# Output products of three mixers, their last two column chunks taken by halves of the tokens, with the next norm and first product also by halves

## The chip, the cores and the metric

The kernel runs on one core of a Trainium2 chip. The metric is the device time of one execution in microseconds (us), the median of several executions. An engine's name in the profile is short: PE is the matrix engine (PEld its weight loads), DVE the vector engine, ACT the scalar engine, POOL the general engine, SP the engine that issues most transfers.

## The reference

Two networks run one after the other over 512 tokens of 1024 features, in 32-bit floats. Cut to what matters here, the order of work is this:

```python
h, gate = adaln_norm(x, ...)                 # mixer 1: norm, scale and shift
x = x + gate * (nsa_mixer(h) @ w_out)        # 16 heads, three branches
h, gate = adaln_norm(x, ...)                 # mixer 2
x = x + gate * (dilated_mixer(h) @ w_out)    # 16 heads in three groups
x = rms_norm(x, final_g)                     # end of the first network
h = modulate(rmsnorm(x, g1), shift1, scale1) # mixer 3: window attention and a short convolution
x = x + gate1 * (merged @ w_out)
h2 = modulate(rmsnorm(x, g2), shift2, scale2)
x = x + gate2 * peer(h2, ...)                # 16384 experts, 8 heads x 16 picked for each token
```

Each norm needs the sum of squares over all 1024 features of a token, so all four column chunks of the output product before it. A token's norm needs nothing of the other tokens.

## The kernel before, in words

Tokens are four tiles of 128 (`NT`), features eight blocks of 128 (`KD`), weights come in chunks of 256 columns (`CW`). The running `x` stays on the chip with tokens on the partitions. Every operand of a large product is split into a high and a low part, and `mm3` (L229) issues three matmuls for one block of 128 features: high with high, high with low, low with high (L230 to L232). A weight chunk is fetched by `load_raw` and split by `load_split` (L220): the high part on ACT (L225), the low part, as raw minus high, on DVE (L226). The split parts live in a pool of two (`wsp`), the raw chunks in a pool of three.

The builder doesn't keep the order in which the program is written: a planner arranges each engine's instructions by a time that it computes for itself, keeping the data's dependences. `behind(...)` (L174) adds an order by hand: an instruction is issued after a named earlier one of its engine. `load_split` uses it for its two instructions unless `wait=False`: they stay behind the last square sum ("stats"), the last split of the norm ("scaled") and, in mixer 3, behind the last split of the convolution branch ("hi" on ACT, "scaled" on DVE, L1105).

The stretch between two mixers, called a join below, is made of three parts:

- The output product of the mixer before: `proj_out` (L446) for mixer 1, loops at L926 for mixer 2 and L1132 for mixer 3. For each of four column chunks c and each token tile t there are 24 matmuls of 256 columns (27 in mixer 2, whose three head groups are summed apart). The result is scaled by the gate, added to `x` (`add_x`, L439), and ACT sums the squares (L321). For c = 3 and t of 2 or 3, DVE does the adds; else POOL does. In mixer 2, `x` is also multiplied by the final weights (L945) and a second sum of squares follows.
- The norm, `adaln` (L350): `rstd_x` (L323) forms an inverse root with a chain of small DVE instructions, for tiles 0 and 1 and for tiles 2 and 3; `y` is the scaled `x` (L372 on DVE, L370 on ACT); PE transposes y in 128 by 128 blocks (L399, 32 of them); one feature block of all 512 tokens is scaled and shifted on DVE or ACT (L404, L402) and split into the parts `hTh` on ACT (L347) and `hTl` on DVE (L348). The norm ahead of the experts also transposes the first token tile back (L410, L411).
- The first product of the next mixer: two blocks of 24 matmuls of 512 columns (mixer 2 and the experts' queries, `gemm_T`, L234), or four token tiles of 24 matmuls of 256 columns (mixer 3, `gemm_N`, L248). Its weights are split with `wait=False`.

PSUM tiles come from pools: `mm` (two), `ss` (three), `tt` (two, tiles named tps), `oo` (one). `bank(t)` (L244) takes tiles 0 and 1 from mm, 2 and 3 from ss. In mixer 2 the third group's sums of two token tiles share one tps tile (L932).

## Time and profile before

| | us |
|---|---|
| median of 3 runs | 2246.64 |
| lowest and highest run | 2243.02, 2252.53 |
| the profiled execution, device time | 2243.89 |
| its span, first to last instruction | 2241.9 |
| PE busy | 2153.9 (96% of the span) |
| DVE busy | 1726.8 (77%) |
| ACT busy | 993.2 (44%) |
| POOL busy | 583.0 (26%) |

The span lies 2.0 us under the device time. Busy shares are means over the whole span. Times below are microseconds from the start of the span. A matmul's length in a timeline includes the time in the pipe, so the distance between two starts tells the pace.

### The profile page before, as it was taken

The page shows a single profiled execution, that of the slowest core. Times are in us where ns is not written, and L with a number is a line of the kernel's source. Part 1 is how long each engine was busy: PE and PEld are TensorE (multiplying, and loading weights), DVE is VectorE, ACT ScalarE, POOL GpSimd, SP SyncE. Part 2 cuts the span into 40 slices and gives each one's busy share as a digit, 9 for nine tenths or more (in the row PEclk, how much of TensorE's full clock was granted, in tenths as well). Part 3 has the DMA queues.
Part 4 walks back from the last instruction along what each step waited for, and adds up shares of the span by engine and source line. Part 5 has one row for each costly group of instructions (what it writes and reads, how often), then busy time and mean ns, then how long its engine had stood idle before and what let it go on. Part 6 is the DMA issues. An engine that isn't in the chain of part 4 may idle for free.

```text
span 2241.9 us, 33090 instructions
## 1 busy us (share of the span) xinstructions
PE 2153.9 (96%) x12587; PEld 1858.0 (83%) x12587; DVE 1726.8 (77%) x3499; ACT 993.2 (44%) x1756; POOL 583.0 (26%) x385
## 2 busy tenths in 40 slices
PE   6989999999999899989999999899999999999998
PEld 4877776977787787788899999788888888888887
DVE  6676788488765587659899998678777878788785
ACT  4435666344555544353344877533233333333331
POOL 1231100211010711110000002245545536435450
PEclk9999999999999999999999999999999999999999
DMA  7541120145441142134445569899999989999993
GB/s 292 204 154 51 38 76 20 57 155 189 158 161 66 67 153 76 39 111 147 153 150 203 217 260 349 326 371 341 349 327 339 361 309 360 333 332 353 335 355 128
DMA packets 151824, 474.38 MB, mean 212 GB/s; under 512 B 14321, under 2 KB 66417, under 8 KB 128625
## 3 DMA queue, kind: packets, MB, share of 16 engines
q1 hardware_dynamic: 108464, 300.28, 37.4%
q0 software_dynamic: 36864, 134.23, 15.8%
q10 hardware_dynamic: 6336, 37.75, 4.3%
q8 instruction: 99, 1.62, 0.3%
q14 instruction: 61, 0.49, 0.1%
HBM read 429.76 MB, written 41.94 MB: 210 GB/s over the span
## 4 chain that ended last, share of the span: by engine, by line
PE 87%; DVE 6%; ACT 2%; DMA 2%; POOL 1%; issue 1%; SPq 0%; ACTq 0%; DVEq 0%; POOLq 0%
PE mmps L230 15%; PE mmps L232 15%; PE mmps L231 15%; PE sp L232 5%; PE sp L230 5%; PE sp L231 5%; PE sp L493 3%; PE tps L231 3%; PE tps L230 3%; PE tps L232 3%; PE tps L517 2%; PE ob L741 2%; DVE adacc L271 2%; PE ob L230 1%; PE ob L232 1%; PE ob L231 1%
## 5 line engine op out<-in xcount | busy, mean ns | idle before, releaser
L230 PE MATMUL mmps<-hTh,whi 128*128 128x384 f32 (+1 forms) x1656 | 600.8, 364 | 6.1 <-ACT pa L1191 2.5
L231 PE MATMUL mmps<-hTl,whi 128*128 128x384 f32 (+1 forms) x1656 | 596.1, 360 | 3.4 <-DVE hTl L348 3.4
L232 PE MATMUL mmps<-hTh,wlo 128*128 128x384 f32 (+1 forms) x1656 | 594.9, 360 | 1.3 <-DVE wlo L226 1.3
L1204 POOL DMA_INDIRECT rows<-in_un_dram,idx x128 | 205.7, 1607 | 595.3 <-DVE rows L1209 336.0
L230 PEld LDWEIGHTS mmps<-hTh,whi 128*128 128x128 f32 x1656 | 312.4, 189 | 38.4 <-ACT pa L1191 3.7
L231 PEld LDWEIGHTS mmps<-hTl,whi 128*128 128x128 f32 x1656 | 313.0, 189 | 31.6 <-DVE hTl L348 5.1
L232 PEld LDWEIGHTS mmps<-hTh,wlo 128*128 128x128 f32 x1656 | 312.5, 189 | 29.4 <-DVE wlo L226 1.6
L225 ACT ACTIVATE whi<-wr 128x2048 fp32r<-128x2048 f32 x121 | 230.2, 1903 | 142.1 <-PE mmps L231 90.3
L226 DVE TENSOR_TENSOR wlo<-wr,whi 128x2048 fp32r<-128x2048 f32 x111 | 252.7, 2277 | 35.5 <-ACT whi L225 35.0
L1204 POOL DMA_INDIRECT rows<-in_v_dram,idx x128 | 198.7, 1552 | 212.1 <-DVE acc L1223 170.0
L1461 DVE TENSOR_TENSOR vl<-wr,vh 128x2048 fp32r<-128x2048 f32 x64 | 146.5, 2290 | 124.7 <-ACT vh L1452 112.0
L1452 ACT ACTIVATE vh<-wr 128x2048 fp32r<-128x2048 f32 x64 | 122.4, 1915 | 258.4 <-PE ob L232 240.2
L271 DVE SCALAR_TENSOR_TENSOR adacc<-wr,c_c,adacc 128x256 f32<-128x256 f32 x308 | 164.5, 552 | 3.2
L1223 DVE SCALAR_TENSOR_TENSOR acc<-rows,dots,acc 128x1024 f32<-128x1024 f32 x127 | 162.6, 1280 | 1.6
L1209 DVE SCALAR_TENSOR_TENSOR rows<-rows,hn 128x1024 f32<-128x1024 f32 x128 | 153.1, 1217 | 7.7 <-DMA rows<-in_un_dram,idx 7.5
L230 PE MATMUL sp<-vh,wh 128*128 128x512 f32 x384 | 144.9, 394 | 10.0 <-ACT wh L1464 10.0
L231 PE MATMUL sp<-vl,wh 128*128 128x512 f32 x384 | 148.7, 393 | 0.0
L232 PE MATMUL sp<-vh,wl 128*128 128x512 f32 x384 | 136.8, 390 | 0.4 <-DVE wl L1465 0.4
L1464 ACT ACTIVATE wh<-pa 128x768 fp32r<-128x768 f32 x64 | 53.1, 842 | 153.6 <-DVE pa L1463 94.5
L231 PE MATMUL tps<-vl,wh 128*128 128x512 f32 x256 | 100.0, 393 | 0.0
L230 PE MATMUL tps<-vh,wh 128*128 128x512 f32 x256 | 98.5, 393 | 0.0
L232 PE MATMUL tps<-vh,wl 128*128 128x512 f32 x256 | 95.0, 389 | 0.0
(1100 smaller groups left out, 4196.8 us busy)
## 6 DMA issues: line engine op xcount, KB each, us to landing
wr<-in_u_dram SPq DMA_DIRECT2D x64, 1024.0 KB, 7.3
wr<-in_v_dram SPq DMA_DIRECT2D x64, 1024.0 KB, 8.3
wr<-in_aw_dram SPq DMA_DIRECT2D x48, 1024.0 KB, 6.6
gd<-stg ACTq DMA_DIRECT2D x12, 2048.0 KB
pg<-gd SPq DMA_DIRECT2D x32, 768.0 KB, 9.7
wr<-in_dilw_dram SPq DMA_DIRECT2D x16, 1024.0 KB, 4.8
ad<-aout ACTq DMA_DIRECT2D x32, 384.0 KB, 2.8
pa<-ad SPq DMA_DIRECT2D x32, 384.0 KB, 9.2
```

The costliest lines, as they stand in the source:

```text
L225: A.activation(hi[:, :, :n], r[:, :, :n], AF.Copy)
L226: (lo_eng or V).tensor_tensor(lo[:, :, :n], r[:, :, :n], hi[:, :, :n].bitcast(F32), op=ALU.subtract)
L230: TE.matmul(ps, sh, mh, start=first, stop=False)
L231: TE.matmul(ps, sh, ml, start=False, stop=False)
L232: TE.matmul(ps, sl, mh, start=False, stop=last)
L271: V.scalar_tensor_tensor(acc, r[:, k, :], m.ccol[:, k:k + 1], acc, op0=ALU.mult, op1=ALU.add)
L493: TE.matmul(sp[j], q, k, start=False, stop=True, skip_group_check=True)
L1204: G.indirect_dma_start(out=r, out_offset=None, in_=table, in_offset=bass.IndirectOffsetOnAxis(ap=ix, axis=0))
L1209: V.scalar_tensor_tensor(r, r, 1.0, hn, op0=ALU.mult, op1=ALU.mult, accum_out=dots[:, n:n + 1])
L1223: V.scalar_tensor_tensor(acc, r, dots[:, n:n + 1], acc, op0=ALU.mult, op1=ALU.add)
L1452: A.activation(vh, vr, AF.Copy)
L1461: paced(V.tensor_sub(vl, vr, vh.bitcast(F32)))
```

## The change

The output product of each of the three mixers keeps chunks 0 and 1 as they were. Chunks 2 and 3 are both loaded and split ahead, and then run for token tiles 0 and 1 (both chunks) and then for tiles 2 and 3. The norm of tiles 0 and 1 is written between chunk 2 and chunk 3 of tiles 2 and 3. The first product of the next mixer is written for the first half of the tokens, then the norm of the second half, then the product of the second half. `adaln_halves` takes the norm's pool while the product before still runs; so the pools of the attention are closed earlier (`ast`), and what outlives them moves (`al`, `fg`, `o5`). The norm writes into the tiles that the output product reads in mixers 1 and 2 (`oT`), at the columns of its own half. `first` holds the first product in two mm tiles until both halves are in. In mixer 2 each token tile takes a tps tile of its own. The chunk-0 split of mixer 3's output product loses its `wait=c > 0`. The back-transposition ahead of the experts becomes `natural`, after the second head's scores. The diff, cut to its core:

```diff
+    def gemm_T_half(hT, w, pss_, half):
+        hs = slice(half * (T // 2), (half + 1) * (T // 2))
+        for b, ps in enumerate(pss_):
+            sl = slice(b * P, (b + 1) * P)
+            for k in range(KD):
+                mm3(ps[:, hs], w[0][:, k, sl], w[1][:, k, sl], hT[0][:, k, hs], hT[1][:, k, hs], k == 0, k == KD - 1)
...
+    def adaln_halves(st, hT, sh, sc, g, fin=False):
+        npool = pool("nrm", 1, st)
+        y = npool.tile([P, NT, D], F32, name="y")
...
+        def half(t0):
+            r, r1 = rstd_x(fin, t0, t0 + 2)
+            for t in (t0, t0 + 1):
+                if t % 2:
+                    A.activation(y[:, t, :], x[:, t, :], AF.Copy, scale=r[:, t - t0:t - t0 + 1])
+                else:
+                    V.tensor_scalar(y[:, t, :], x[:, t, :], r[:, t - t0:t - t0 + 1], None, op0=ALU.mult)
+            hs = slice(t0 * P, (t0 + 2) * P)
+            for k in range(0, KD, 2):
+                src = (pst.tile([P, 2, 2 * P], F32, name="tps", tag="tps") if k % 4 == 0 else pss.tile([P, 2, 2 * P], F32, name="sp", tag="sp"))
+                for j in range(2):
+                    for t in (t0, t0 + 1):
+                        TE.transpose(src[:, j, (t - t0) * P:(t - t0 + 1) * P], y[:, t, (k + j) * P:(k + j + 1) * P], ident)
+                f = npool.tile([P, 2, 2 * P], F32, name="hf", tag="hf", bufs=2)
+                V.tensor_scalar(f[:, 0], src[:, 0], a_[:, k:k + 1], sh.out[:, k:k + 1], op0=ALU.mult, op1=ALU.add)
+                A.activation(f[:, 1], src[:, 1], AF.Identity, scale=a_[:, k + 1:k + 2], bias=sh.out[:, k + 1:k + 2])
+                last["scaled"] = split(hT[0][:, k:k + 2, hs], hT[1][:, k:k + 2, hs], f)
+            if fin:
+                with behind("scaled"):
+                    for t in (t0, t0 + 1):
+                        G.tensor_scalar(x[:, t, :], x[:, t, :], r1[:, t - t0:t - t0 + 1], None, op0=ALU.mult)
+        return half
...
+    def two_halves(wname, step, half):
+        v_ = chunks(i[wname], [CW] * 4)
+        for c in range(2):
+            w = load_split(*v_[c])
+            for t in range(NT):
+                step(t, c, w)
+        w = [load_split(*v_[c]) for c in (2, 3)]
+        for t0 in (0, 2):
+            for c in (2, 3):
+                for t in (t0, t0 + 1):
+                    step(t, c, w[c - 2])
+                if t0 and c == 2:
+                    half(0)
...
-        proj_out(oT, "nsawo", gate.out)
         st.close()
+        half = adaln_halves(nrm, oT, shift[1], scale[1], ng[1])
+        proj_out(oT, "nsawo", gate.out, half)
...
         w0 = load_split(*ch[0], wait=False)
-        hT = adaln(shift[1], scale[1], ng[1])
+        hT = hT1
+        first = [psm.tile([P, T], F32, name="mmps", tag="mm") for _ in range(2)]
+        gemm_T_half(hT, w0, first, 0)
+        half1(2)
+        nrm.close()
...
+        ast.close()
+        half = adaln_halves(st, oT, sh1, sc1, n1g, fin=True)
+        fgp = pool("fgp", 1, st)
+        o5 = [fgp.tile([P, T], F32R, name="o5" + n) for n in "hl"]
+        own_half(o5, zT[:, SPL, :], 1)
+        fg = fgp.tile([P, D], F32, name="fg")
         S.dma_start(fg, i["fg"].to_broadcast([P, D]))
...
-                pa_ = bank(t)
-                if t % 2 == 0:
-                    pb_ = pst.tile([P, T], F32, name="tps", tag="tps")
-                pg = [pa_[:, :CW], pa_[:, CW:], pb_[:, (t % 2) * CW:(t % 2 + 1) * CW]]
+            pa_ = bank(t + 2 * c & 3)
+            pb_ = pst.tile([P, T], F32, name="tps", tag="tps")
+            pg = [pa_[:, :CW], pa_[:, CW:], pb_[:, :CW]]
...
+        two_halves("dilwo", step, half)
+        ch = chunks(i["b2w"], B2_W)
+        w0 = load_split(*ch[0], wait=False)
+        first = [psm.tile([P, T], F32, name="mmps", tag="mm") for _ in range(2)]
+        for t, ps in enumerate(first):
+            gemm_N_tile(oT, w0, CW, ps, t)
+        half(2)
         st.close()
...
-        for c, v_ in enumerate(chunks(i["b2wo"], [CW] * 4)):
-            w = load_split(*v_, wait=c > 0)
+        ast.close()
+        hn_ = new_hT()
+        half = adaln_halves(st, hn_, sh2, sc2, n2g)
...
+        two_halves("b2wo", step, half)
+        w0 = load_split(*chunks(i["wq"], [CW] * 8)[0], wait=False)
+        first = [psm.tile([P, T], F32, name="mmps", tag="mm") for _ in range(2)]
+        gemm_T_half(hn_, w0, first, 0)
+        half(2)
         st.close()
...
+    def natural():
+        for k in range(0, KD, 4):
+            hs = rw.tile([P, 4, P], F32, name="hs", tag="oho")
+            V.tensor_tensor(hs, hT[0][:, k:k + 4, 0:P].bitcast(F32), hT[1][:, k:k + 4, 0:P].bitcast(F32), op=ALU.add)
+            ps = pst.tile([P, T], F32, name="tps", tag="tps")
+            for j in range(4):
+                TE.transpose(ps[:, j * P:(j + 1) * P], hs[:, j, :], ident)
+            A.activation(hn[:, k * P:(k + 4) * P], ps, AF.Copy)
```

## Rows read from the trace of the kernel before

**Rows 1.** The page's chain that ended last: shares of the span by engine

```profile
PE 87%; DVE 6%; ACT 2%; DMA 2%; POOL 1%; issue 1%; SPq 0%; ACTq 0%; DVEq 0%; POOLq 0%
```

**Rows 2.** PE's waits at joins 1, 2, 3: total us, times, longest us

```profile
PE tps L399 <- DVE y L372: 3.5, 2, 3.2
...
PE tps L399 <- DVE y L372: 8.5, 2, 7.7
...
PE tps L399 <- DVE y L372: 4.7, 2, 2.7
```

**Rows 3.** Windows of join 1: PE, PEld, DVE, ACT, POOL busy, PEclk, DMA share, GB/s

```profile
450.00:455.00 5.00, 1.83 (x14) 1.59 (x12) 2.96 (x14) 3.46 (x4) 0.00 (x0) 0.85 0.34 107
455.00:460.00 5.00, 4.95 (x20) 4.16 (x19) 2.92 (x5) 3.24 (x6) 0.00 (x0) 0.50 0.01 3
460.00:465.00 5.00, 5.00 (x26) 4.19 (x25) 3.94 (x6) 3.19 (x6) 0.00 (x0) 0.97 0.23 75
```

**Rows 4.** Timeline, PE, join 1: start us, length us, engine, line, tile

```profile
448.96 0.28 PE L232 MATMUL sp<-whi,hTl 128*128 128x256 f32 x1
...
471.01 0.39 PE L232 MATMUL mmps<-hTh,wlo 128*128 128x512 f32 x1
```

**Rows 5.** Timeline, PE, join 2: last matmuls of chunk 3, tiles 1 and 3

```profile
768.12 0.28 PE L232 MATMUL tps<-whi,hTl 128*128 128x256 f32 x1
...
771.71 0.28 PE L232 MATMUL tps<-whi,hTl 128*128 128x256 f32 x1
```

**Rows 6.** Timeline, DVE and ACT, join 2: y of each half, fourth tile's evacuation

```profile
778.87 0.75 DVE L372 TENSOR_SCALAR y<-x,nr 128x1024 f32<-128x1024 f32 x1
...
782.08 1.15 ACT L370 ACTIVATE y<-x,nr 128x1024 f32<-128x1024 f32 x1 [1.14 <-DVE nr L201]
...
803.40 0.39 ACT L1011 ACTIVATE qk<-mmps 128x256 f32<-128x256 f32 x1 [2.49 <-PE mmps L232]
```

**Rows 7.** Timeline, PE, join 3: end of output product and of first product

```profile
986.01 0.28 PE L232 MATMUL sp<-whi,mTl 128*128 128x256 f32 x1
...
1011.07 0.39 PE L232 MATMUL mmps<-hTh,wlo 128*128 128x512 f32 x1
```

**Rows 8.** The chain in order of time: start us, us, what (joins 1, 2)

```profile
461.90 0.23 PE mmps L232
462.13 0.44 PE sp L399 x4
...
796.63 0.12 PE mmps L231
```

**Rows 9.** Timeline, ACT: second half's y at joins 1 and 3

```profile
453.25 1.15 ACT L370 ACTIVATE y<-x,nr 128x1024 f32<-128x1024 f32 x1 [0.60 <-DVE nr L201]
...
991.89 1.15 ACT L370 ACTIVATE y<-x,nr 128x1024 f32<-128x1024 f32 x1 [0.59 <-DVE nr L201]
```

**Rows 10.** Instructions of tile hf: durations ns, minimum, median, maximum

```profile
L347 ACT ACTIVATE hTh<-hf x32: 612/619/633, 33.9 to 1008.0; 128x512 fp32r<-128x512 f32 x32
L348 DVE TENSOR_TENSOR hTl<-hf,hTh x32: 678/691/1164, 38.7 to 1008.7; 128x512 fp32r<-128x512 f32 x32
```

**Rows 11.** Timeline, ACT and DVE, join 1: split of the next mixer's first weights

```profile
437.76 1.92 ACT L225 ACTIVATE whi<-wr 128x2048 fp32r<-128x2048 f32 x1 [1.02 <-PE sp L232]
...
439.71 2.29 DVE L226 TENSOR_TENSOR wlo<-wr,whi 128x2048 fp32r<-128x2048 f32 x1 [1.45 <-ACT whi L225]
```

**Rows 12.** Timeline, ACT and PE, ahead of mixer 3's output product

```profile
927.89 1.92 ACT L225 ACTIVATE whi<-wr 128x2048 fp32r<-128x2048 f32 x1 [0.41 <-PE mmps L231]
...
939.05 0.39 PE L232 MATMUL mmps<-hTh,wlo 128*128 128x512 f32 x1
...
940.74 0.71 ACT L1102 ACTIVATE mTh<-cy,c_og 128x512 fp32r<-128x512 f32 x1
```

**Rows 13.** Timeline, DVE: group weights of mixer 2 become ready

```profile
730.37 0.17 DVE L920 TENSOR_TENSOR al<-al,gm 128x12 f32<-128x12 f32 x1
```

**Rows 14.** Timeline, POOL, join 2: x scaled by the final norm

```profile
779.73 11.75 POOL L377 TENSOR_SCALAR x<-x,nr 128x1024 f32<-128x1024 f32 x4 [5.05 <-DVE rs_a L197]
```

More of the change, by code (lines that the diff above doesn't have):

```diff
@@ L795, in group_stats, with own_half @@
             V.tensor_scalar(st0[:, :, 1, g], st0[:, :, 1, g], 1.0 / nh, None, op0=ALU.mult)
+        def own_half(dst, f, h):
+            split(dst[0][HS[h]], dst[1][HS[h]], f[HS[h]])
+            for z in dst:
+                A.activation(z[HS[1 - h]], zero[HS[1 - h]].to_broadcast([64, T]), AF.Copy)
         def gated(k):
@@ L800, in gated @@
             if k == SPL:
-                for dst, own, other in ((0, HS[0], HS[1]), (1, HS[1], HS[0])):
-                    hi, lo = [oT[j][:, k, :] if dst == 0 else o5[0][:, j, :] for j in range(2)]
-                    split(hi[own], lo[own], f[own])
-                    for z in (hi, lo):
-                        A.activation(z[other], zero[other].to_broadcast([64, T]), AF.Copy)
+                own_half([z[:, k, :] for z in oT], f, 0)
+                V.tensor_copy(zT[HS[1], k, :], f[HS[1]])
                 return
@@ L821, in ev @@
                     rope_T(tmp, dst[:, b, :], scl, wk, tab, rotr, None if 4 * c + 2 * b < NP else (bycls, inorder))
-                gemm_T(hT, w, 2, ev)
+                if c + cc:
+                    gemm_T(hT, w, 2, ev)
+                else:
+                    gemm_T_half(hT, w, first, 1)
+                    for b in range(2):
+                        ev(b, first[b])
                 ada_next()
@@ L926, in dil, with step @@
[L926 to L927 removed]
+        src = lambda g, k, j: o5[j] if (g, k) == (2, SPL) else oT[j][:, k, :]
+        def step(t, c, w):
             csl = slice(c * CW, (c + 1) * CW)
[L929 to L948 removed]
@@ new lines, in step @@
+            tsl = slice(t * P, (t + 1) * P)
+            pa_ = bank(t + 2 * c & 3)
+            pb_ = pst.tile([P, T], F32, name="tps", tag="tps")
+            pg = [pa_[:, :CW], pa_[:, CW:], pb_[:, :CW]]
+            for g in range(3):
+                for k in rows[g]:
+                    mm3(pg[g], src(g, k, 0)[:, tsl], src(g, k, 1)[:, tsl], w[0][:, k, :], w[1][:, k, :], k == rows[g][0], k == rows[g][-1])
+            tmp = sm.tile([P, CW], F32, name="po", tag="adacc")
+            A.activation(tmp, pg[0], AF.Copy, scale=al[:, t, 0:1])
@@ new lines, in step @@
+            for g in (1, 2):
+                V.scalar_tensor_tensor(tmp, pg[g], al[:, t, g:g + 1], tmp, op0=ALU.mult, op1=ALU.add)
+            eng = V if c == 3 and t >= 2 else G
+            eng.tensor_tensor(tmp, tmp, gate.out[:, csl], op=ALU.mult)
+            add_x(t, c, tmp, eng)
+            eng.tensor_tensor(x[:, t, csl], x[:, t, csl], fg[:, csl], op=ALU.mult)
+            q = square_sum(t, c, 1)
+            if c == 3:
+                last["stats"] = q
+        two_halves("dilwo", step, half)
@@ L1130, in mixer2, with step @@
         rsqrt_(rr, rv, 2 * NT)
[L1132 to L1133 removed]
+        ast.close()
+        hn_ = new_hT()
+        half = adaln_halves(st, hn_, sh2, sc2, n2g)
+        def step(t, c, w):
             csl = slice(c * CW, (c + 1) * CW)
[L1135 to L1149 removed]
@@ new lines, in step @@
+            tsl = slice(t * P, (t + 1) * P)
+            ps = bank(t + 2 * c & 3)
+            pp = [ps[:, :CW], ps[:, CW:]]
+            for hf in range(2):
+                for k in range(4 * hf, 4 * hf + 4):
+                    src = (aT, mT)[hf]
+                    mm3(pp[hf], src[0][:, k % 4, tsl], src[1][:, k % 4, tsl], w[0][:, k, :], w[1][:, k, :], k % 4 == 0, k % 4 == 3)
+            tmp = sm.tile([P, CW], F32, name="po", tag="adacc")
+            A.activation(tmp, pp[0], AF.Copy, scale=rr[:, t:t + 1])
@@ new lines, in step @@
+            t2 = sm.tile([P, CW], F32, name="po", tag="adacc")
+            V.scalar_tensor_tensor(t2, pp[1], rr[:, 4 + t:5 + t], tmp, op0=ALU.mult, op1=ALU.add)
+            t3 = sm.tile([P, CW], F32, name="po", tag="adacc")
+            (V if c == 3 and t >= 2 else G).tensor_tensor(t3, t2, gate.out[:, csl], op=ALU.mult)
+            add_x(t, c, t3, V)
+        two_halves("b2wo", step, half)
+        w0 = load_split(*chunks(i["wq"], [CW] * 8)[0], wait=False)
+        first = [psm.tile([P, T], F32, name="mmps", tag="mm") for _ in range(2)]
@@ L1150, in mixer2 @@
+        gemm_T_half(hn_, w0, first, 0)
+        half(2)
         st.close()
-    mixer2()
+        return hn_, w0, first
+    hT, wq0, first3 = mixer2()
     NH, TK = 8, 16
@@ L1284, in ev @@
             V.tensor_scalar(ids[:, :, m, :], ix, 128.0 if b == 0 else 1.0, None, op0=ALU.mult)
-        gemm_T(hT, w, 2, ev)
+        if h:
+            gemm_T(hT, w, 2, ev)
+        else:
+            gemm_T_half(hT, w, first3, 1)
+            for b in range(2):
+                ev(b, first3[b])
+    def natural():
[6 more added lines that the diff above has]
+            A.activation(hn[:, k * P:(k + 4) * P], ps, AF.Copy)
     def route(t):
@@ L1392, in body @@
         scores(h)
+        if h == 1:
+            natural()
         if h % 2:
```

101 lines of the change are left out of this document (37 added, 64 removed).

## Prediction

> **What bounds the kernel now.** I read the chain that ended last first: 87% of the span is PE [rows 1], so time is won only where PE stands still or runs slowly. PE's waits, asked around the three joins (mixer 1 to 2, 2 to 3, 3 to the experts), show what holds it there: the transposes wait for y, 3.5, 8.5 and 4.7 us [rows 2]. The windows of the first join show a second price: after PE's 3.2 us wait the granted clock goes from 1.0 to 0.85 and then 0.50, that is from 2.4 to 1.2 GHz, and is back at 0.97 only in the window after 460 [rows 3]. So a join is more than its wait; I measure it from the last matmul of the output product to the end of the next mixer's first product.
>
> For the ends I need PE's paces, and the chain in order of time gives them: 0.23 us for a matmul of 512 columns, 0.12 for one of 256, 0.44 for four transposes, so 0.11 each [rows 8].
>
> - Join 1: 448.96 + 0.12 = 449.08 to 471.01 + 0.23 = 471.24 is 22.2 us [rows 4, 8].
> - Join 2: 771.71 + 0.12 = 771.83 to the evacuation of the fourth tile at 803.40, some 0.2 after its last matmul, is 31.4 us [rows 5, 6].
> - Join 3: 986.13 to 1011.30 is 25.2 us [rows 7, 8].
>
> PE's own work in each, at full pace, is 32 transposes (3.5 us) and 48 matmuls of 512 columns (11.0) or 96 of 256 (11.5), and in join 3 eight more transposes (0.9): 14.5, 15.0 and 15.4 us. The joins lose 7.7 + 16.4 + 9.8 = 33.9 us, 1.5% of the time. No change of their order can bring more than that.
>
> **The change part by part.**
>
> *The second half's chain.* With the halves, PE has the first half's product to do (48 matmuls of 256 columns, 48 x 0.12 = 5.8 us) while the second half's norm runs. What ends last is then that norm. From the last matmul to the end of y on ACT before: 453.25 + 1.15 - 449.08 = 5.3 us in join 1, 782.08 + 1.15 - 771.83 = 11.4 in join 2, 991.89 + 1.15 - 986.13 = 6.9 in join 3 [rows 4 to 7, 9]. In join 2 the root chains of both halves stood interleaved on DVE; y of the first half began at 778.87, that of the second at 782.08 [rows 6]. With the first half long done I take 2 us off: 9.4. From y to the first matmul: four transposes 0.44, a scaling of 256 columns out of PSUM about 0.39 (an estimate by the 256-column evacuation on ACT [rows 6]), the high split 0.62 [rows 10], and some 0.3 for hand-overs: 1.8 us. Then 5.8 us of matmuls, and 0.5 because the low part comes 0.69 after the high [rows 10]: 6.3. A pair of blocks costs ACT about 0.39 + 0.62 and DVE about the same + 0.07, under PE's 1.44 for its 12 matmuls, so the split keeps up.
>
> *What the first half adds.* Its 16 transposes (1.8 us) move in front of the join's end; that is no saving, and I add them. Its norm must fit under the product of tiles 2 and 3, four tiles of 2.9 us (3.2 in mixer 2). Queued on DVE in these 11.6 us: the splits and scalings of four pairs (4 x (0.69 + 0.39) = 4.3), a root chain (twelve small steps, of the size of the 0.17 of [rows 13], 2.4 with what lies between them), y (0.75 [rows 6]), eight evacuations and adds of 256 columns (some 3, estimated at 0.39 each), and the next weights' low split (2.29). That last one is what is tight: before, the split of w0 began when chunk 2 let go of its buffer, took 1.92 on ACT and then 2.29 on DVE, and had all of chunk 3, 11.6 us, as cover [rows 11]. Now chunk 2 ends only 5.8 us ahead of the end. ACT and DVE come out at 13 us of work for 13 us of time, so I book 1 us of lateness per join (bounds 0 and 4). In join 2 the first half's y came 778.87 - 768.24 = 10.6 us after its last matmul [rows 5, 6], while only 6.5 us of tiles 2 and 3 of chunk 2 lie between. I book nothing, because the chunk-3 tiles' first two head groups (36 x 0.12 = 4.3 us) need no tps tile and can go first; if they don't, the cost is 4.1 us and a clock that falls.
>
> The joins after: join 1, 1.8 + 5.3 + 1.8 + 6.3 + 1 = 16.2 (gain 6.0); join 2, 1.8 + 9.4 + 1.8 + 6.3 + 1, and 1 for a clock that falls in the some 5 us that stay uncovered = 21.3 (gain 10.1); join 3, 1.8 + 6.9 + 1.8 + 6.3 + 1 = 17.8 (gain 7.4). Together 23.5 us, bounds 14 and 29.
>
> *The lost `wait=c > 0`.* Before, the high split of mixer 3's first output weights ran at 927.89, ahead of the last convolution product, which ended at 939.28; the convolution's high split on ACT came at 940.74 to 941.45 [rows 12]. The new loop keeps every chunk behind that instruction, so this split can't end before 941.45 + 1.9 = 943.35. PE, which went on without a break, has nothing for 943.35 - 939.28 = 4.1 us, more than the wait that brought the clock down in join 1 [rows 2, 3]. Some 4 us of work at 1.2 GHz adds 2. Behind this split stand the low split (DVE, 2.29) and the group of small root steps that the evacuations wait for; four PSUM tiles of work cover those. Cost 6 us, bounds 0 and 8.
>
> *A tps tile for each token tile in mixer 2.* The four third-group sums of chunk 0 fitted into two tiles and ran before their weights `al` were ready at 730.5 [rows 13]; now the third and fourth must wait for an evacuation. 18 x 0.12 = 2.2 us of work can't go ahead; I take 1.5 us, bounds 0 and 3. After that the tiles turn over every 6.5 us, longer than an evacuation behind a low split (some 4).
>
> *Edits at nothing.* `natural` takes 8 transposes out of join 3 and puts them, with two DVE adds, into the scores; PE's work there is the same, and that is in the sum. The two splits at chunk 2 and 3: the second gets its buffer at chunk 1's end and has two tiles, 5.8 us, for 4.2 [rows 11]; without that cover, up to 4 us per mixer. `o5` and `fg` move to memory that attention frees; `fg` is first read after chunk 0, but its transfer stands on SP's queue, where the raw weights go too: 0 if the planner puts it behind them.
>
> *POOL's scaling of x.* It ran from 779.73 for 11.75 us, four instructions of 2.9 [rows 14], beside the second half's chain. DVE's low splits went from 0.69 to at most 1.16 [rows 10]. Now two of the four run in the same place, and I book nothing more. The Trainium skill ("SBUF — State Buffer", "Who interferes with whom") says that a DVE instruction with two SBUF inputs and a GpSimd instruction that reads SBUF exclude one another for the whole instruction; no row here shows such a full block, and the second rival is priced from POOL's row.
>
> The sum: 23.5 - 6 - 1.5 = 16 us off the profiled execution's 2243.9, so 2227.9. The median lies 2.75 above that execution, so 2230.6 on the scale of the median; I say 2230. Nothing later takes it back: a shorter join only starts the experts earlier.
>
> **The rivals.**
>
> 1. *The wait costs nothing* (0.14). The planner had the weights split early and the hand-made order doesn't bind. For it: nothing but the doubt in how the order is kept. 2224.
> 2. *POOL shuts DVE out* (0.05). Both POOL instructions of the first half fall into join 2's second chain and each holds a DVE instruction for up to 2.9 us: 5.8 more, 2236. Against it: the 1.16 above. The page named there would have it so.
> 3. *The first half isn't covered* (0.17). Join 2 pays 4.1 and 3 for the clock, and the three joins are each 1 us later for DVE's queue: 10 us, 2240. For it: the 10.6 us; against it: the two groups that can go first.
> 4. *The planner undoes it* (0.05). It sets the first half's norm behind the whole output product; the joins stay, the two costs come: 2254.
> 5. *Slower: the clock falls twice in each join* (0.07). If PE stands for over 3 us already ahead of the first half's product, waiting for w0 behind DVE's queue, that product runs at 1.2 GHz: 5.8 us more. It is too short to bring the clock back (before, PE worked through the window from 455 to 460 at 0.50 [rows 3]), PE stops again, and the second product pays 5.8 too. 11.6 in three joins less the 1 booked is 34: 2264. It decides at a wait of about 3 us; I have booked 1.
>
> **How the numbers follow.** Some 0.5%, 11 us, is what a measurement of this kernel can tell from no change. The forecast (0.52) and rival 1 lie beyond it on the fast side: 0.66. Rivals 2, 3 and 4 lie within: 0.27. Rival 5: 0.07. The range goes from 2218 (rival 1 with joins at their lower bounds) to 2246 (rival 3 with the wait's upper bound and the tps tiles'), and leaves out rivals 4 and 5 and a little below.
>
> **What the new profile would show.** PE's waits for y at the joins fall from 16.7 us to under 8, almost all at join 2. The joins measure about 16, 21 and 18 us by the same marks. Ahead of mixer 3's output product PE waits some 4 us for an ACT split at L225, with a clock of 0.5 after it. The forecast is wrong if PE waits for L226 or L348 ahead of the first half's product, if the clock is at 0.5 through a whole join, or if transposes of the first half stand on PE waiting while chunk-3 matmuls could run.

## Result, and the profile after

The changed kernel takes 2259.26 us in the median (2255.14 to 2264.94), the kernel before beside it 2246.14: a ratio of 1.0056, interval 1.0040 to 1.0072. It is slower; the forecast was 2230.

The profiled execution of after took 2264.94 us (span 2261.6), the longest of its runs; that of before 2243.89 (span 2241.9). PE's share of the chain that ended last, by engine, went from 87% [rows 1] to 84%:

```profile
PE 84%; DVE 7%; ACT 3%; DMA 3%; issue 2%; POOL 1%; SPq 0%; ACTq 0%; DVEq 0%; POOLq 0%
```

Two profiled executions can't be compared by their clock times: output product 1 begins at 416.8 us before and at 423.0 after, with nothing changed up to there. So I cut both at the same instructions: the first evacuation of output product 1; the first evacuation of mixer 2's key product; the exponential of mixer 2's group weights (`al`); the first evacuation of mixer 3's values; the convolution's last square in mixer 3; the first and the last evacuation of the experts' query scores. Stage lengths in us, with the sum's forecast for each change:

| stage | before | after | change | forecast |
|---|---|---|---|---|
| join 1 | 54.2 | 52.3 | -1.8 | -6.0 |
| middle of mixer 2 | 258.3 | 260.7 | +2.4 | 0 |
| output product 2 and join 2 | 88.7 | 96.4 | +7.7 | -8.6 (10.1 less 1.5) |
| middle of mixer 3 | 122.2 | 125.0 | +2.8 | 0 |
| output product 3 and join 3 | 70.8 | 72.8 | +2.0 | -1.4 (7.4 less 6) |
| scores | 119.5 | 120.4 | +0.9 | 0 |

The changes add up to 14.0 (the medians differ by 13.1), the forecast to -16. Of the 30 us between them 16.3 lie in join 2.

What PE waited for in join 2 and on the way to it, after (total us, times, longest), beside [rows 2]:

```profile
PE tps L446 <- DVE y L440: 9.4, 2, 6.1
...
PE sp L546 <- ACT hf L449: 3.1, 1, 3.1
PE tps L230 <- ACT o5h L867: 2.2, 1, 2.2
...
PE mmps L230 <- ACT qk L1093: 0.7, 1, 0.7
```

The same waits in PE's timeline (start, length, and in brackets the idle time ahead and what ended it):

```profile
737.59 0.58 PE L230 MATMUL tps<-whi,o5h 128*128 128x256 f32 x1 [2.21 <-ACT o5h L867]
...
778.84 0.28 PE L232 MATMUL mmps<-whi,hTl 128*128 128x256 f32 x1
...
785.18 0.47 PE L446 MATMUL tps<-c_ident,y 128*128 128x128 f32 x1 [6.06 <-DVE y L440]
...
793.44 0.28 PE L232 MATMUL tps<-whi,hTl 128*128 128x256 f32 x1
...
808.39 0.58 PE L546 MATMUL sp<-c_masks,c_identb 128*128 128x512 bf16 x1 [3.09 <-ACT hf L449]
...
809.71 0.58 PE L230 MATMUL mmps<-whi,hTh 128*128 128x256 f32 x1 [0.73 <-ACT qk L1093]
```

Windows of after (columns as in [rows 3]): each wait is followed by a stretch in which PE has work at the lower clock, 0.50 being 1.2 GHz.

```profile
735.00:740.00 5.00, 2.79 (x15) 2.71 (x15) 3.71 (x14) 3.42 (x8) 0.00 (x0) 0.59 0.00 0
...
780.00:785.00 5.00, 0.00 (x0) 0.00 (x0) 4.93 (x13) 2.10 (x8) 2.12 (x1) 0.87 0.28 88
785.00:790.00 5.00, 4.82 (x23) 4.83 (x24) 1.90 (x4) 2.69 (x5) 4.78 (x2) 0.50 0.29 123
...
805.00:810.00 5.00, 1.18 (x4) 0.43 (x4) 3.48 (x7) 3.57 (x8) 1.75 (x1) 0.76 0.00 2
810.00:815.00 5.00, 5.00 (x27) 5.00 (x27) 4.76 (x15) 0.04 (x1) 0.00 (x0) 0.55 0.29 79
```

By the forecast's own marks join 2 did shrink: 793.44 + 0.12 = 793.56 to the fourth tile's evacuation at 817.83 is 24.3 us (31.6 before to the same mark; the forecast took 0.2 off). The loss stands ahead of that mark: from the exponential of `al` to the last output matmul it was 771.83 - 729.30 = 42.5, and now 793.56 - 736.02 = 57.5, 15.0 more: the wait for y 6.1, for `o5` 2.2, the first half's 16 transposes 1.8, 16 matmuls of the first product that now run ahead of the mark 1.9, and a rest of 3.0 that I put down to the lower clock.

### The profile page after: what moved, and what is told of

The parts are those of the page before. It is cut to its first block, busy times and chain, and to the rows that moved or that the text cites. A ratio compares the mean times of both kernels' runs of the same rounds, so it can differ in the third digit from the quotient of the medians.

```text
span 2261.6 us, 33325 instructions
## 1 busy us (share of the span) xinstructions
PE 2167.2 (96%) x12683; PEld 1873.9 (83%) x12683; DVE 1733.5 (77%) x3505; ACT 996.1 (44%) x1762; POOL 581.8 (26%) x385
## 4 chain that ended last, share of the span: by engine, by line
PE 84%; DVE 7%; ACT 3%; DMA 3%; issue 2%; POOL 1%; SPq 0%; ACTq 0%; DVEq 0%; POOLq 0%
PE mmps L230 14%; PE mmps L232 14%; PE mmps L231 14%; PE sp L230 5%; PE sp L232 5%; PE sp L231 5%; PE tps L230 3%; PE tps L231 3%; PE sp L552 3%; PE tps L232 3%; PE tps L576 2%; PE ob L800 2%; DVE adacc L284 2%; PE ob L230 1%; PE ob L232 1%
## 5 line engine op out<-in xcount | busy, mean ns | idle before, releaser
L230 PE MATMUL mmps<-hTh,whi 128*128 128x384 f32 (+2 forms) x1688 | 607.2, 361 | 10.3 <-ACT hTh L360 6.1
L231 PE MATMUL mmps<-hTl,whi 128*128 128x384 f32 (+2 forms) x1688 | 603.9, 358 | 5.2 <-DVE hTl L361 5.1
L232 PE MATMUL mmps<-hTh,wlo 128*128 128x384 f32 (+2 forms) x1688 | 602.1, 358 | 2.5 <-DVE wlo L226 2.5
L230 PEld LDWEIGHTS mmps<-hTh,whi 128*128 128x128 f32 x1688 | 319.3, 190 | 42.7 <-ACT hTh L360 7.6
L231 PEld LDWEIGHTS mmps<-hTl,whi 128*128 128x128 f32 x1688 | 320.3, 190 | 33.3 <-DVE hTl L361 7.5
L232 PEld LDWEIGHTS mmps<-hTh,wlo 128*128 128x128 f32 x1688 | 320.1, 190 | 30.9 <-DVE wlo L226 3.3
L1558 ACT ACTIVATE vh<-wr 128x2048 fp32r<-128x2048 f32 x64 | 122.5, 1915 | 286.5 <-PE ob L232 260.2
```

Source lines behind the costliest of these rows:

```text
L230: TE.matmul(ps, sh, mh, start=first, stop=False)
L231: TE.matmul(ps, sh, ml, start=False, stop=False)
L232: TE.matmul(ps, sl, mh, start=False, stop=last)
L1558: A.activation(vh, vr, AF.Copy)
```

## Experiments

### Which join

The theory drawn from these rows was that join 2 alone makes the kernel slower and that the other two gain little; the rivals, that each join loses, or that the lost `wait=c > 0` does. Each join was changed alone, the others written as before, and join 3 also with the wait argument back for the chunk-0 split of mixer 3's output product:

```diff
-            w = load_split(*v_[c])
+            w = load_split(*v_[c], wait=c > 0 or wname != "b2wo")
```

> Only join 1 (mixer 1 to 2) in halves; mixers 2 and 3 and the experts written as before. Theory A, the places: in the two traces join 1 took 1.9 us off, but mixer 2 behind it came out 3.5 us longer with the same work; if that loss belongs to join 1, this kernel is within 3 us of the kernel before (2244 to 2249); if it belongs to join 2's new memory plan, it is 2 us faster than before (2242 to 2245). Theory B, the clock falls twice in each join: a third of the whole loss of 13 us, so 4 us slower (2250).

> Only join 2 (mixer 2 to 3) in halves. Theory A: this is where the time went. From the last of mixer 2's attention to the first evacuation behind the join the trace of after has 7.7 us more than before; 7 to 11 us slower than before (2253 to 2257). Theory B: a third of the loss, 2250.

> Only join 3 (mixer 3 to the experts) in halves, with the first weights of mixer 3's output product kept behind the convolution branch as in after. Theory A: the join wins 4.8 us (25.2 before, 20.4 in the trace of after) and the start of the output product loses about 6: 1 to 3 us slower than before (2247 to 2249). Theory B: 2250.

> As j3_alone, but the first weight chunk of mixer 3's output product is split without the hand-made wait, as in the kernel before. If the lost wait costs what I booked, 6 us, this is 6 us faster than j3_alone, some 4 to 5 us faster than before (2241 to 2243). If the hand-made order does not bind, the two are the same.

| kernel | median us | ratio to before | interval | stage of its join |
|---|---|---|---|---|
| j1_alone | 2246.76 | 1.0002 | 0.9989 to 1.0015 | 52.4 |
| j2_alone | 2258.91 | 1.0050 | 1.0035 to 1.0064 | 96.3 |
| j3_alone | 2248.89 | 1.0008 | 0.9996 to 1.0020 | 72.1 |
| j3_alone_w | 2242.57 | 0.9985 | 0.9976 to 0.9994 | 67.1 |

Join 2 holds the whole loss: 12 us by the medians, more than the 7 to 11 expected. The lost wait costs 6.3 us by the medians and 5.0 by the stage. Join 1's 1.8 us don't reach the end: at about 515 us PE waits 1.2 us in j1_alone for a low split that it didn't wait for before. The same wait in after:

```profile
PE mmps L232 <- DVE wlo L226: 1.3, 1, 1.3
```

### What in join 2

Three causes stood in the rows. (a) The third-group sums of the chunk-3 tiles take tps tiles in the order of the program, behind the first half's transposes, which wait for y; PE, in order, stands with ready work behind it. (b) The first product's tiles 2 and 3 take the two mm tiles of tiles 0 and 1, whose evacuations stand on ACT behind the second half's high splits, and a mask matmul (L546) ahead of them waits for the last `hf`. (c) `o5` is now split behind the exponential of `al` on ACT. One edit for each:

```diff
 (a) j2_sp
-                src = (pst.tile(...) if k % 4 == 0 else pss.tile(...))
+                src = (pst.tile(...) if k % 4 == 0 and not fin else pss.tile(...))
 (b) j2_bank, in the first product of mixer 3
-                ps = bank(0)
+                ps = bank(t if made else 0)
 (c) j2_o5: close ast, take o5 and split it right behind the third group's statistics, ahead of al
```

> Join 2 alone in halves, and o5 with its two splits and two zero copies written ahead of the chain of al, so that ACT's queue has them before al's exp. Theory T3, o5 is late: in the trace of j2_alone PE waits 2.21 us for o5 and then goes at half pace for some 5 us; without it 3 to 5 us less than j2_alone's 2258.9, so 2254 to 2256. Rival R, the time of the join is set by DVE's chain to y alone: the output product ends earlier but y waits for its own squares, which also come earlier; the same 3 to 5. If the third-group sums wait for al anyway, nothing: 2259.

> Join 2 alone in halves, with the transposes of both halves in sp tiles, none in tps. Theory T1, a tps tile blocks: the two third-group sums of chunk 3 (18 matmuls each, 4.3 us) then run ahead of the transposes, into the 5.93 us in which PE waits for y, and the clock falls later or not at all: 5 to 7 us less than j2_alone, 2252 to 2254. Rival R, DVE's chain sets the time: PE gets its 4.3 us of work done and waits the same time later, for the second y; 0 to 2 us less, 2257 to 2259.

> Join 2 alone in halves, with tiles 2 and 3 of the first product in sp tiles, so that they need no evacuation of tiles 0 and 1. Theory T2, the second half's product waits for its tiles: in j2_alone it starts at 805.94 behind waits of 3.09 (for the last hf) and 0.73 us (for the evacuation) and runs at half pace at first; here it can start with the first split pair, some 3 us earlier, and overlap the splits: 3 to 5 us less than j2_alone, 2254 to 2256. Rival R: the same start, 2259.

> The three edits together. If the three waits are separate causes the gains add: 11 to 17 us less than j2_alone, 2242 to 2248, so the same as the kernel before or 5 us faster. If DVE's chain to y sets the time (rival R), only o5's part stays: 2254 to 2256.

> Join 2 alone in halves, with o5's early splits and the transposes in sp tiles, tiles 2 and 3 of the first product as in after. In the traces the stretch from al to the ninth qk evacuation is 99.1 us in j2_alone, 95.7 with o5 early, 94.6 with sp. If the two add, it is 91.2 here, as in the kernel before (91.4), and the time 2246 to 2248. The order of mixer 3's attention is that of the kernel before, so the 15 us that j2_all3's profiled run lost there (clock 0.50 from 882 to 912) should not occur. If that loss comes with join 2 in halves whatever the order, some of the runs are 10 us and more above the rest, as in j2_all3.

| kernel | median us | ratio | interval | join 2's stage |
|---|---|---|---|---|
| j2_alone | 2258.91 | 1.0050 | 1.0035 to 1.0064 | 96.3 |
| j2_o5 | 2254.19 | 1.0023 | 1.0009 to 1.0037 | 93.0 |
| j2_sp | 2249.97 | 1.0006 | 0.9994 to 1.0018 | 91.9 |
| j2_bank | 2249.93 | 1.0006 | 0.9992 to 1.0019 | 90.8 |
| j2_o5_sp | 2251.25 | 1.0024 | 1.0011 to 1.0036 | 87.6 |
| j2_all3 | 2251.25 | 1.0024 | 1.0004 to 1.0045 | 86.2 |

Each cause is real: 3.3, 4.4 and 5.5 us of the stage by itself (by the medians 4.7, 8.9 and 9.0), and 10.1 together where the sum is 13.2.

The wait for the first half's y itself stays: 5.3 us in j2_sp, 7.5 in j2_o5_sp and j2_all3 (7.7 before). What edit (a) gives is that the last output sums no longer stand behind it, so that the second half's y comes 4.2 us earlier after `al`.

With all three the stage is 2.5 below before's 88.7, and the whole kernel isn't faster, against the 2242 to 2248 expected; nor is j2_o5_sp (expected 2246 to 2248), whose stage is 1.1 below before's and whose middle of mixer 3 takes 127.5 us, with PE's order as before. In j2_all3's profiled execution (2260.2; its runs go from 2245.1 to 2266.6) the gain and more went in mixer 3's attention, 139.9 us for 122.2: one wait of 1.9 us for `pt` at 880, and then thirty microseconds in which PE is never idle, at 1.2 GHz:

```profile
872.40:882.40 10.00, 8.13 (x48) 5.64 (x47) 5.54 (x20) 5.73 (x19) 0.00 (x0) 0.96 0.01 2
882.40:892.40 10.00, 10.00 (x30) 5.73 (x29) 5.20 (x22) 3.58 (x15) 0.00 (x0) 0.50 0.28 105
892.40:902.40 10.00, 10.00 (x38) 6.37 (x38) 4.90 (x24) 6.05 (x22) 0.00 (x0) 0.50 0.00 0
902.40:912.40 10.00, 10.00 (x41) 6.26 (x42) 4.73 (x21) 1.11 (x5) 0.00 (x0) 0.50 0.00 0
```

There the planner had ordered the attention differently. But the fall comes without that too, as the next runs show.

### All joins, mended

after_fix3 is the changed kernel with the wait argument back, `o5` early and the transposes in sp tiles alone; j13_w has joins 1 and 3 with the wait argument; j13_w_tiles gives each of a pair's two scalings an output tile and a split of its own:

```diff
-                f = npool.tile([P, 2, 2 * P], F32, name="hf", tag="hf", bufs=2)
+                f0, f1 = [npool.tile([P, 2 * P], F32, name=n, tag=n, bufs=2) for n in ("hf", "hg")]
...
```

> Joins 1 and 3 in halves with the wait restored, join 2 as in the kernel before. If the joins are independent, j1_alone's 0 and j3_alone_w's -4.3 add: 2242 to 2244. If join 2 in halves had been needed by its neighbours or join 1's loss of 1 to 2 us in mixer 2's middle counts, 2245 to 2247.

> As j13_w, but the two scaled blocks of a pair are two tiles with a split each. In join 1 ACT's scaling started when DVE's of the same tile ended (456.31 after 455.73 + 0.54), so the first matmul came 3.4 us after the transposes where I booked 1.8. If the shared tile makes ACT wait, the first matmul of each half comes some 1 us earlier: 2 to 4 us less than j13_w over two joins and two halves, 2238 to 2241. If ACT waits for something else, the four more instructions for a pair cost: 0 to 2 us more than j13_w.

> The kernel after with three edits: the wait restored, o5's splits ahead of al's chain, and the transposes of join 2 in sp tiles. By the single runs, after's 2259.3 less 6.3 (the wait), less 4.7 (o5) and less 8.9 (sp) if all add: 2240; with the two of join 2 adding only to the join's 8 us: 2244 to 2246.

j13_w: 2244.61, 0.9990 (0.9979 to 1.0000). j13_w_tiles: 2243.24, 0.9985 (0.9972 to 0.9997). after_fix3: 2241.68, 0.9981 (0.9968 to 0.9993): faster than both kernels, by 4.5 and 17.6 us. Its stages are 52.3, 259.9, 87.6, 121.4, 68.2 and 120.4; against before that makes 3.9. j13_w_tiles can't be told from j13_w, so the two theories of its expectation stay undecided by the time; its trace is read below.

In the middle of mixer 3, j13_w and j13_w_tiles issue the same instructions in the same order and PE's waits are the same (0.8, 0.8 and 0.9 us); the stage is 122.4 in the one and 125.7 in the other. Two windows of j13_w:

```profile
913.00:918.00 5.00, 4.06 (x30) 3.00 (x31) 4.93 (x10) 1.32 (x2) 0.00 (x0) 1.00 0.02 3
918.00:923.00 5.00, 5.00 (x33) 3.88 (x32) 0.00 (x0) 0.00 (x0) 0.00 (x0) 1.00 0.00 0
```

and a window of j13_w_tiles, whose work is 3.9 us earlier by the clock time, so that it begins with what j13_w does at 916.9:

```profile
913.00:918.00 5.00, 5.00 (x14) 3.99 (x15) 1.35 (x2) 0.00 (x0) 0.00 (x0) 0.52 0.00 0
```

The stage is 121.4 to 122.5 in before, j1_alone, j3_alone, j3_alone_w, j13_w and after_fix3, 123.2 in fix3_alt, and 123.9 to 126.5 in after and ten of the experiments, before_fill among them, which changes nothing near it; j2_o5_sp and j2_all3 lie above. So I don't put the table's +2.8 down to the change, though no run shows what decides it.

### The split's own pace

In the second half of join 3 a pair of blocks takes DVE and ACT 1.71 us (two in 3.42), over PE's 1.44. Timeline of DVE and ACT, after:

```profile
1021.47 0.55 DVE L448 TENSOR_SCALAR hf<-tps,amod,sh 128x256 f32<-128x256 f32 x1 [0.21 <-PE tps L446]
...
1023.68 1.29 DVE L361 TENSOR_TENSOR hTl<-hf,hTh 128x512 fp32r<-128x512 f32 x2 [1.21 <-ACT hTh L360]
1024.89 0.54 DVE L448 TENSOR_SCALAR hf<-tps,amod,sh 128x256 f32<-128x256 f32 x1
...
1025.53 0.57 ACT L449 ACTIVATE hf<-tps,sh,amod 128x256 f32<-128x256 f32 x1 [1.36 <-DVE hf L448]
```

ACT's scaling starts when DVE's of the same PSUM tile ends (1024.89 + 0.54, then 1025.53), and the program has a semaphore wait there. Separate output tiles didn't free it (j13_w_tiles: DVE's 460.23 + 0.54, ACT's at 460.87), so what they share is the PSUM tile. The Trainium skill ("PSUM — Partial Sum Buffer", "PSUM bank collisions raise a hardware error ⚠️") has it that two engines must not access a bank in the same partitions at once; the wait agrees with it. fix3_alt, on after_fix3, gives both scalings of a pair to one engine and the next pair to the other; on fix3_alt, alt_hf4 adds two more `hf` buffers, and alt_pool gives POOL the low split of the next weights at joins 1 and 3, to take 2.29 us off DVE; fix3_y, on after_fix3, holds the next weights' split back behind the first half's y instead, and fix3_y_alt does that on fix3_alt.

```diff
 fix3_alt
-                V.tensor_scalar(f[:, 0], src[:, 0], ...)
-                A.activation(f[:, 1], src[:, 1], ...)
+                for j in range(2):
+                    if k % 4: A.activation(f[:, j], src[:, j], ...)
+                    else: V.tensor_scalar(f[:, j], src[:, j], ...)
 fix3_y: last["y"] set at y on DVE, and at all three joins
-        w0 = load_split(*ch[0], wait=False)
+        w0 = load_split(*ch[0], wait=("y",))
 alt_hf4: hf bufs=4        alt_pool: load_split(..., lo_eng=G)
```

> after_fix3, with the two scalings of a pair on one engine, DVE for the tps pairs and ACT for the sp pairs, instead of one on each. Theory E, two engines read one tile of sums one after the other: ACT's scaling started at the end of DVE's in every pair (in j13_w_tiles with two output tiles as well), so a pair took 1.1 us and both engines waited for one another; with a whole pair on one engine two pairs go side by side. The first matmul of a half comes at the same time, the later pairs some 1 us earlier: 1 to 3 us less than after_fix3 over three joins, 2239 to 2241. Rival: the splits set the pace, not the scalings; 2242.

> after_fix3, with the split of the next mixer's first weights kept behind the first half's y. In the trace of after_fix3 the low split (2.28 us) stands inside the first half's root chain at joins 2 and 3: at join 3 the chain takes 7.2 us from nv at 977.80 to nr at 984.99, and PE waits 2.35 us for y and runs at half pace after it. Theory D, DVE's queue holds the first half up: y comes some 2 us earlier at both joins, 2 to 5 us less than after_fix3's 2241.7, so 2237 to 2240. Rival: the low split is then late for the first product by as much, 2241 to 2243.

> Both edits. If both theories hold, 3 to 7 us less than after_fix3: 2235 to 2239. If neither does, 2242.

> fix3_alt with four hf buffers instead of two. In after_fix3 the second half's pairs at join 3 go in rounds of 3.42 us for two pairs (DVE's scalings at 993.16, 996.57 and 999.99): DVE scales, ACT scales and takes the high parts, DVE takes the low parts, and only then are the buffers free for the next scalings; each engine idles 1.2 to 1.4 us in a round. Theory F, this lockstep, 1.71 us for a pair where PE's 12 matmuls take 1.44, holds the joins: with four buffers the halves' chains are 1 to 2 us shorter each, 2 to 5 us less than fix3_alt's 2242.9, 2238 to 2241. Rival: the engines then take all scalings ahead of the first split, the first matmul is later by as much, 2242 to 2244.

> fix3_alt with the low split of the first weights behind joins 1 and 3 on POOL instead of DVE. Theory D again, without the delay that fix3_y brought to those weights: DVE's root chain of the first half at join 3 (7.2 us in after_fix3) is free of the 2.28 us, y comes 2 us earlier and PE's wait for it (2.35 us) goes: 2 to 4 us less than fix3_alt's 2242.9, 2239 to 2241. Rival: POOL's pass over 2048 columns (some 4.6 us by its like in the windows of the first mixer) slows DVE beside it by as much: 2243.

| kernel | median us | ratio | interval | joins 1, 2, 3 |
|---|---|---|---|---|
| after_fix3 | 2241.68 | 0.9981 | 0.9968 to 0.9993 | 52.3, 87.6, 68.2 |
| fix3_alt | 2242.91 | 0.9977 | 0.9966 to 0.9989 | 51.7, 88.1, 66.0 |
| fix3_y | 2248.07 | 0.9998 | 0.9988 to 1.0009 | 52.4, 89.7, 67.5 |
| fix3_y_alt | 2248.00 | 1.0000 | 0.9985 to 1.0014 | 51.7, 90.7, 67.0 |
| alt_hf4 | 2246.40 | 1.0000 | 0.9990 to 1.0009 | 53.1, 88.3, 68.2 |
| alt_pool | 2249.02 | 1.0013 | 1.0002 to 1.0024 | 52.6, 89.3, 69.5 |

One engine a pair shortens joins 1 and 3 by 0.7 and 2.2 us, though join 3 with one code varies from 67.1 to 68.2 between kernels; two pairs then take 2.96 us instead of 3.42. As a whole fix3_alt can't be told from after_fix3. Holding the split back lost 2.1 at join 2, and 4 us in all by the ratios (6 by the medians): a remedy that failed. PE's waits for y did shrink, from 6.6 to 2.4 us at join 2 and from 2.3 to none at join 3, but waits for the halves' scalings and splits took their place. More buffers lost 1.4 and 2.2 against fix3_alt: all scalings then go ahead of the first split. alt_pool shows why its idea fails. POOL and DVE, alt_pool, at joins 1 and 3 (0.43 and 0.16 are the usual lengths of the two DVE instructions):

```profile
453.21 4.62 POOL L226 TENSOR_TENSOR wlo<-wr,whi 128x2048 fp32r<-128x2048 f32 x1 [0.73 <-POOL x L488]
...
454.50 3.60 DVE L488 TENSOR_TENSOR x<-x,po 128x256 f32<-128x256 f32 x1
...
994.54 4.71 POOL L226 TENSOR_TENSOR wlo<-wr,whi 128x2048 fp32r<-128x2048 f32 x1 [0.47 <-DVE rs_a L197]
...
994.74 4.53 DVE L199 TENSOR_TENSOR rs_b<-rs_a,rs_y 128x2 f32<-128x2 f32 x1
```

A root step of two elements took 4.53 us: it ended with POOL's instruction (994.54 + 4.71 = 999.25, 994.74 + 4.53 = 999.27).

### Was it PE's clock

before_fill is the kernel before with matmuls that nobody reads behind the last product of each join (28, 64 and 40), so that PE doesn't stand still:

```diff
+            for _ in range(n):
+                TE.matmul(ob[:, :CW], w[0][:, 0, :P], w[0][:, 0, :], start=True, stop=True)
```

> The kernel before, with matmuls of the first weights by themselves into a tile that nobody reads, between the last matmul of each output product and the first transposes: 28, 64 and 40 of 256 columns (3.4, 7.7 and 4.8 us). PE stays busy through most of its wait. Theory C, the clock is a price of its own: the windows of 0.85 and 0.50 at join 1 and their like at the others go, and each join is 1.5 to 3 us shorter: 4 to 8 us less than before, 2238 to 2242. Rival: the chain of scalings and splits sets the join's end and the clock costs nothing there: 2245 to 2247.

2247.61, 0.9996 (0.9981 to 1.0011). Windows of join 2 in before_fill:

```profile
773.00:778.00 5.00, 4.93 (x42) 4.73 (x41) 4.56 (x26) 3.94 (x11) 0.47 (x1) 1.00 0.35 110
778.00:783.00 5.00, 3.03 (x18) 2.53 (x16) 3.12 (x9) 2.12 (x3) 5.00 (x2) 0.78 0.00 0
783.00:788.00 5.00, 4.84 (x32) 3.86 (x30) 3.56 (x5) 3.41 (x6) 5.00 (x3) 0.88 0.00 0
```

and those of before in the same stretch (the work comes 2.2 us later there):

```profile
775.00:780.00 5.00, 0.32 (x2) 0.32 (x3) 4.39 (x27) 3.94 (x12) 0.27 (x1) 0.50 0.34 107
780.00:785.00 5.00, 4.15 (x19) 3.36 (x18) 3.12 (x9) 2.12 (x3) 5.00 (x2) 0.50 0.00 0
785.00:790.00 5.00, 4.95 (x32) 4.54 (x31) 3.56 (x5) 3.60 (x6) 5.00 (x3) 0.70 0.00 0
```

The clock was 1.00, 0.78 and 0.88 where it had been 0.50, 0.50 and 0.70, and join 2 measures 88.7, as before. So at join 2 the lower clock cost next to nothing before: what ends it is the chain of norm, scaling and split on DVE and ACT, and the half-pace product ran inside that.

Join 1 is another case: there the clock has a price. The stage is 51.8 in before_fill, 2.3 below before, and eight microseconds of it, in before, in j3_alone_w (join 1 as before there, stage 53.0) and in before_fill, are these:

```profile
452.83:460.83 8.00, 6.71 (x26) 5.80 (x27) 4.83 (x9) 4.79 (x7) 0.00 (x0) 0.57 0.01 4
...
458.60:466.60 8.00, 6.51 (x31) 5.45 (x32) 5.53 (x11) 5.08 (x8) 0.00 (x0) 0.79 0.01 3
...
452.52:460.52 8.00, 7.15 (x48) 5.85 (x46) 5.52 (x11) 5.07 (x8) 0.00 (x0) 1.00 0.01 3
```

In the nine kernels whose join 1 is unchanged the stage goes from 52.8 to 54.2, the shorter ones with the higher clock. In halves it is 52.3 at a clock of 1.00: the halves gained there no more than a clock kept up by dead matmuls does, so it isn't shown that working by halves, and not the clock, won the table's 1.8. At join 3, where unchanged kernels measure 70.4 to 71.9, before_fill measures 70.1 and halves with the wait back 67.1 to 68.2; there the gain is more than the clock's.

## Why the prediction was wrong

**Where PE stands, and that this is where time is won**: right as an observation, but the bound was loose. "The joins lose (...) 33.9 us" took every stop and slow stretch of PE as its loss; before_fill removes much of the slow stretch at join 2 and gains nothing there.

**"I book nothing, because the chunk-3 tiles' first two head groups (...) can go first"**: the step that failed most. They did go first, the last at 778.84. But I asked only which work needs no tps tile and not what stands behind the transposes in the queue for one: the third-group sums. The first half's y came at 784.37 + 0.75 = 785.12, and PE waited 6.06 us and went on at half pace. This was named as what would make the forecast wrong, and rival 3, whose condition came true at join 2, had its price (4.1 and 3, at 0.17); j2_sp bears the mechanism out with 4.4 us of the stage.

**The first half's norm.** That y was so late is a term of its own, and it made most of the wait. Of the sixteen third-group sums the twelfth is the last of the first half:

```profile
769.52 0.28 PE L232 MATMUL tps<-whi,hTl 128*128 128x256 f32 x1
...
784.37 0.75 DVE L440 TENSOR_SCALAR y<-x,nr 128x1024 f32<-128x1024 f32 x1
```

From 769.64 to y it took 14.7 us, where the prediction took over 10.6 from the trace before; PE's other work covered 9.3 of it, up to 778.96, where 6.5 + 4.3 = 10.8 were booked. Counted from the exponential of `al`, the last matmul moved 5.3 us forward and y only 1.2 (49.6 to 48.4): the work on DVE, ACT and POOL behind it set y's time. From `nv` to `nr` the first half's root chain took 784.17 + 0.16 - 775.29 = 9.0 us at join 2, the second half's 800.05 - 796.84 = 3.2. Rows of DVE and POOL, after, in that chain:

```profile
777.37 0.73 DVE L192 TENSOR_SCALAR rs_h<-nv 128x4 int32<-128x4 int32 x1
...
778.96 0.71 DVE L199 TENSOR_TENSOR rs_b<-rs_a,rs_y 128x4 f32<-128x4 f32 x1
...
779.98 2.29 DVE L226 TENSOR_TENSOR wlo<-wr,whi 128x2048 fp32r<-128x2048 f32 x1
...
780.74 2.12 POOL L1019 TENSOR_TENSOR x<-x,fg 128x256 f32<-128x256 f32 x1 [1.08 <-ACT sqs L334]
```

The next weights' low split stands in the middle of it, as feared ("what is tight"), and small steps beside POOL's adds take 0.7 instead of 0.17. I had booked 1 us for all of DVE's queue, by 13 us of work for 13 us of time (at joins 1 and 3 the time is 11.6 by the same paragraph); that the first half's chain runs in the busiest stretch of DVE and POOL had no price.

**`o5` and the mm tiles.** `o5` "at nothing" failed: 2.21 us of PE's wait, 3.3 of the stage (j2_o5). I weighed its memory, not that its split now stands behind the pool it frees and so behind `al`'s chain on ACT. That the product of the second half must wait for the evacuation of the first half's two tiles had no term; 5.5 of the stage (j2_bank).

**The second half's chain, and "the split keeps up".** Join 1 after, on PE:

```profile
456.88 0.28 PE L232 MATMUL mmps<-whi,hTl 128*128 128x256 f32 x1
...
468.87 0.50 PE L230 MATMUL mmps<-hTh,whi 128*128 128x256 f32 x2 [0.19 <-ACT hTh L360]
...
475.62 0.28 PE L232 MATMUL mmps<-hTh,wlo 128*128 128x256 f32 x1
```

From the last output matmul (457.00) to y's end on ACT (463.50 + 1.16) it is 7.7, booked 5.3 and 1; from there to the second half's first matmul 4.2, booked 1.8; then 6.9, booked 6.3. With the first half's 1.8 of transposes that is 20.6 for 16.2, and the gain 1.6 to 1.8 instead of 6.0, no more than before_fill's clock gives. PE does the first half's product while the second half's norm runs, as forecast; the sizes didn't hold: a scaling is 0.54 to 0.57 and not 0.39, and the pair's two go one after the other, 1.71 a pair and not under 1.44. Join 3 is 1010.21 to 1030.58, 20.4 us for 25.2 before and 17.8 forecast, by the same terms; there the first half's transposes came only after the whole output product. At join 2 the chain to y's end was shorter than booked, 800.09 + 1.15 - 793.56 = 7.7 for 10.4; but from there to the second half's first matmul at 809.71 it is 8.5, booked 1.8, for cause (b) and the pace of the split, and the product, half of it at the lower clock, took 8.1 to the fourth tile's evacuation.

**The lost wait**: right in size. Booked 6 (bounds 0 and 8), measured 5.0 to 6.3. PE's waits there and two windows, after:

```profile
PE tps L1182 <- ACT csq L1173: 1.3, 1, 1.3
PE sp L230 <- ACT whi L225: 1.1, 1, 1.1
...
PE mmps L230 <- ACT whi L225: 0.7, 1, 0.7
...
960.00:965.00 5.00, 3.43 (x15) 2.94 (x16) 4.90 (x7) 2.25 (x2) 0.00 (x0) 0.62 0.18 43
965.00:970.00 5.00, 5.00 (x32) 5.00 (x32) 1.83 (x10) 0.47 (x1) 0.74 (x1) 0.69 0.92 369
```

They add up to 3.1 us for the 4.1 booked, 1.8 of it for the splits; the rest of the cost I put down to work at the lower clock.

**`natural`**: "PE's work there is the same, and that is in the sum" was wrong by 0.9: the sum took its 8 transposes' 0.9 us as a gain at join 3, and the scores, which PE fills, gave them back (119.5 to 120.4).

**"Nothing later takes it back"**: it does. Join 1's gain meets the wait at 515 us, and mixer 3's attention can lose more than a join's gain, though no run shows that the change decides this.

**The rivals.** Rival 5 had the right side and the wrong reason: at join 2 the clock did fall twice, ahead of the first half's product and ahead of the second's, but by the waits above and not for w0; at join 1 it didn't fall at all, nor at join 3 behind its output product. That its 2264 lies near the measured 2259 is chance. Windows of join 1, after (columns as in [rows 3]):

```profile
455.00:460.00 5.00, 3.86 (x32) 3.45 (x31) 3.70 (x9) 4.18 (x9) 0.00 (x0) 1.00 0.79 288
460.00:465.00 5.00, 4.41 (x35) 4.00 (x34) 3.89 (x15) 3.67 (x6) 0.00 (x0) 1.00 0.10 32
```

Rival 2 was dismissed by "no row here shows such a full block". alt_pool shows one, and after's steps of 0.7 are its small form; POOL's add at 780.74 is held by DVE's split, 2.12 for 0.74. The Trainium skill ("SBUF — State Buffer", "Who interferes with whom") says that a DVE instruction with two SBUF inputs contends with a GpSimd instruction that reads SBUF; the rows in which both the DVE and the POOL (GpSimd) instruction have two inputs agree. For the instruction that rival 2 was about they don't: POOL's scaling of x, with one input, ran from 785.22 for 2.84 us a time, and DVE's low split beside it took its usual 0.69:

```profile
785.22 5.68 POOL L454 TENSOR_SCALAR x<-x,nr 128x1024 f32<-128x1024 f32 x2 [2.37 <-DVE y L440]
...
789.30 0.69 DVE L361 TENSOR_TENSOR hTl<-hf,hTh 128x512 fp32r<-128x512 f32 x1 [1.15 <-ACT hTh L360]
```

Before, the low split that took 1.16 [rows 10] ran at 786.30 beside the same scaling, so it may hold DVE for a part of its length.

**The signs named**: PE's waits for y were to fall to under 8 us; they are 0, 9.4 and 0.6 at the three joins (2.3 at join 3 with the wait back, j3_alone_w, where PE's product ends earlier). Transposes that stand waiting while chunk-3 matmuls could run were to show the forecast wrong, and did.

**Open**: the tps tile for each token tile (1.5 booked) wasn't measured by itself. Whether halves gain anything at join 1 beyond the clock isn't shown. Why the three edits at join 2 leave j2_all3's whole no faster rests on one profiled execution.

## What to carry over

Where a queue is in order and tiles come from a rotating pool, splitting a step in halves puts the late half's producers between ready work and its buffers: list, for each tile that the moved step takes, who takes the next one from that pool, and give the moved step tiles that ready work doesn't need. Price a join by the chain that ends it, not by the engine's idle time; filling that engine with dead work is a cheap way to see which of the two it is, and what the clock alone is worth. And where two engines read halves of one PSUM tile, count their times one after the other.
